# One inference step of a two-layer conv/RWKV-7 decoder on one Trainium2 core: four edits (order of the first activations, where two DVE products are kept, when a chunk and some norms are filled in, how the final squares are summed)

## The chip, the cores and the metric

The kernel runs on one core of one Trainium2 chip. The metric is the time of one execution on the device in microseconds (us). The median of three runs of the kernel before is 2742.42 us (2741.14 to 2746.84). The engines are called PE (matrix products), ACT (activations), DVE (vector), POOL (GpSimd) and SP (issues most DMAs) here, as the profile calls them.

## What is computed

1040 prompt tokens (16 learned meta tokens, then 1024) and 8 decoding tokens pass two layers of width 1024. Layer 0 mixes tokens by a Conformer convolution, layer 1 by RWKV-7; behind each stands an MLP of width 4096 with a squared ReLU, and at the end an RMS norm.

```python
def _wkv7_step(S, inp):                       # one token of RWKV-7, S is 64 x 64 for each of 16 heads
    r_t, w_t, k_t, v_t, kk_t, a_t = inp
    sa = jnp.einsum('bhvk,bhk->bhv', S, -kk_t)
    S = (S * w_t[:, :, None, :] + sa[..., None] * (kk_t * a_t)[:, :, None, :]
         + v_t[..., None] * k_t[:, :, None, :])
    y = jnp.einsum('bhvk,bhk->bhv', S, r_t)
    return S, y
...
    for i in range(DEPTH):                    # DEPTH = 2
        hn = _rmsnorm(h, norm_mix[i])
        if i % N_MIXERS == 0:
            out, buf = _conformer_conv(hn, conv_bufs[j], *[p[j] for p in conv_params])
        else:
            out, sh, S = _rwkv7(hn, shift_bufs[j], wkv_states[j], *[p[j] for p in rwkv_params])
        h = h + out
        h = h + _sqrelu_mlp(_rmsnorm(h, norm_mlp[i]), w_mlp_in[i], w_mlp_out[i])
    return (_rmsnorm(h, norm_final), ...)     # and the new states
```

One of the further outputs, conv_sample, is for each of the 8 decoding sequences the last 30 rows of its convolution buffer: 29 rows of the old state and one new row.

## The kernel before

**Matrix products.** Activations lie with the model dimension on the partitions, 128 of it at a time (KT = 8 blocks), and the tokens in three groups of about 350 columns (352, 348 or 328). Each 1024 x 128 column block of a weight comes by one DMA of 512 KB on SP's queue, in the order in which the program uses them. ACT makes a rounded high part of it (L157, "_hi"), POOL the remainder in four pieces of 128 x 256 (L162, "_lo"). Activations are split in the same way (hn_h and hn_l, m_h and m_l, z_h and z_l, hh and hl). Each product is then three matmuls (L187 high by high, L188 high by low weight, L189 low by high weight), 24 to an output block of 1024 inputs. L354 on DVE adds the output blocks of an MLP ("out") to the residual h.

**Start.** transpose_x loads the first token group, takes its mean square, loads a table of vectors (pvec, tiles stg and ptp), and makes the normalised, transposed activations: PE transposes and scales in one (L486, tile tn), ACT writes hn_h (L488), DVE hn_l (L489). Then pw1 streams the first convolution weights, pg_m (gate) and pa_m (value) in turn, through products ps_g and ps_a. A scheduler of the framework, which goes by its own model of times, orders the instructions here.

**RWKV prompt.** The 1040 tokens go in 17 chunks (16 chunks of 64 tokens and the meta tokens). For every group of chunks inverses() inverts unit triangular 32 x 32 blocks by back substitution on DVE: the blocks ni come by DMA from d_n, then for each column j one product tt (L1172) and one addition to ni (L1173), 30 of each, then ni goes to d_p (L1177) and returns transposed as p (L1200). front() of a chunk loads it and, on DVE, transposes it once more into x (L1203). PE's gg (L1257) is the first product that needs x; behind it come bT, W, po, U, S and Y of the chunk. Products of a group's output projection (ps_oo, residual add L1548) and of its MLP (ps_in, out) are the dense work of the time.

**What sets the order there.** The dense work runs under in_order(): instructions keep the order in which the Python code emits them. A filler() is called between and inside the dense products; it takes further generators in turn (the chunks, the decode step after DL = 74 points, the norms and gates of two token groups) so that each is spread evenly over its points. A generator's yield value is the number of points that it asks to be left alone.

**Decode.** decode_step works the 8 x 16 states as 16 pieces Sdec of 128 x 256. Per piece, DVE does nine instructions (L1406 to L1414): product into t4, reduce to sa, decay of Sdec, product into t4, add (L1410), product into t4, add (L1412), product into t4, reduce to yd. The trace calls the tile t4 "t". Tile t4 lies in SBUF.

**End.** final(g) squares the eight blocks of h on ACT, adds the squares up to two sums (acc_f) on POOL and DVE (L230), sums over partitions with matmuls of one column (L1569, tile fs; two records of the profile each), and takes root and reciprocal (os). PE transposes h (pf), ACT and DVE scale the two halves of a 128-token output tile ot (L1588, L1590), SP stores the tile with one DMA (L1592, L1594). final(1) runs inside the last MLP, final(2) after it.

Eight DMAs on ACT's queue (L1640) copy the old part of conv_sample from DRAM to DRAM. They depend on nothing, and the scheduler issues them in the first 21 us.

Of the kernel before, what the change touches and what calls it, by code (L numbers as in the profile page):

```python
# [8 lines left out]
F32 = mybir.dt.float32  # L9
F32R = mybir.dt.float32r  # L10
# [6 lines left out]
P = 128  # L17
D = 1024
# [30 lines left out]
def hybrid_step(tc, x_prompt, x_sample, state_conv, state_shift, state_wkv, meta_tokens,  # L49
# [10 lines left out]
    with ctx:  # L60
# [9 lines left out]
        for i, e in enumerate((RMS_EPS, LN_EPS, GN_EPS)):  # L70
            nc.vector.memset(eps_t[:, i:i + 1], e)

# [316 lines left out]
        with ExitStack() as l0:  # L389
# [53 lines left out]
            def load_vecs(tiles):  # L443

                for i in tiles:
                    st = cur["raw"].tile([P, D], F32, name=f"stg{i}", tag="raw")[:, :P]
                    nc.gpsimd.memset(st, 0.0)
                    for q, (name, ap) in enumerate(v for v in vecs if col[v[0]] // P == i):
                        r = col[name] % P
                        (nc.gpsimd if q % 2 else nc.scalar).dma_start(st[r:r + ap.shape[0], :], ap)  # L450
                    pt = bank("ptp")
                    nc.tensor.transpose(pt[:, :P], st, ident)
                    nc.vector.tensor_copy(pvec[:, i * P:(i + 1) * P], pt[:, :P])
# [9 lines left out]
            def transpose_x(g, ah, al):  # L463
                n = G0[g][1]
                tiles = load_x(xin, g)
# [12 lines left out]
                if g == 0:  # L478
                    load_vecs([0])
# [13 lines left out]
            def pw1(g, act, fill):  # L493
                n, npr = G0[g][1], prompt_of(g)
                for m in range(KT):
                    wg = load_col(conv_w_pw1[0], KT + m, f"pg{g}_{m}", nc.gpsimd)
                    wa = load_col(conv_w_pw1[0], m, f"pa{g}_{m}", nc.gpsimd)
# [12 lines left out]
                    fill()  # L510
# [26 lines left out]
            def conv_dec(c, c_col):  # L537
# [5 lines left out]
                for m in range(KT):  # L543
# [7 lines left out]
                    nc.vector.tensor_mul(win, win, wdw[:, m:m + 1, :].broadcast_to([P, DEC, CW]))  # L551
                    rd = decp.tile([P, DEC], F32, name=f"rd{m}", tag="rd")
# [119 lines left out]
            with ExitStack() as s:  # L672
# [7 lines left out]
                for _ in transpose_x(0, *acts[0]):  # L680
                    pass
                load_dw()
                for g in range(3):
# [11 lines left out]
                    pw1(g, acts[g], both)  # L695
# [464 lines left out]
        def inverses(c, n):  # L1160
# [7 lines left out]
            top = META if c == 0 else 32  # L1168
            for j in range(top - 2, 0, -1):
                wd = top - 1 - j  # L1170
                o = wk.tile([P, 256], F32, name=f"tt{c}_{j}", tag="tt")[:B, :j * wd].rearrange("p (s t) -> p s t", t=wd)
                nc.vector.tensor_mul(o, ni[:, :j, j:j + 1].broadcast_to([B, j, wd]), ni[:, j:j + 1, j + 1:top].broadcast_to([B, j, wd]))  # L1172
                nc.vector.tensor_add(ni[:, :j, j + 1:top], ni[:, :j, j + 1:top], o)  # L1173
                if j % 4 == 0:
                    yield 1.5
# [55 lines left out]
        fronts = {}  # L1231

# [11 lines left out]
        def chunk(c):  # L1244
# [6 lines left out]
            xa, bk, nr, no, p32, x32 = chunks.pop(c)  # L1251

# [124 lines left out]
        def decode_step():  # L1377

            with ExitStack() as s:
# [135 lines left out]
        with ExitStack() as l1:  # L1515
# [36 lines left out]
            def final(g):  # L1552
                lo, n = G2[g]
                hv = hl[g][:, :, :n]
                accs = mean_parts(hv, n, f"f{g}", True, "facc")
                yield 3
                for k in range(KT):
                    if k % 2:
# [7 lines left out]
                for j, i in enumerate(starts):  # L1566
                    w = min(P, n - i)
                    for q, acc in enumerate(accs):
                        nc.tensor.matmul(ps[:w, j:j + 1], acc[:, i:i + w], ones_d[:, 0:1], start=q == 0, stop=q == 1)  # L1569
# [7 lines left out]
                for j, i in enumerate(starts):  # L1577
# [36 lines left out]
            DL, DN = 74, 90  # L1614

            def late_start(n):
                for _ in range(n):
# [4 lines left out]
                                ([late_start(DL), decode_step()], DL + DN), ([norm_gates(GN_OF[1]), ng2], NGA))  # L1622
# [16 lines left out]
            for q in range(DEC):  # L1639
                nc.scalar.dma_start(o_conv_sample[0, q, 0:CB - 1, :], state_conv[0, q, 1:CB, :])  # L1640
# [46 lines left out]
```

## Time and profile before

| | |
|---|---|
| median of 3 runs | 2742.42 us |
| the profiled execution | 2743.3 us |
| its span, from the first to the last instruction of the trace | 2741.6 us |
| PE busy | 2631.0 us (96%) |
| DVE, ACT, POOL busy | 1727.8, 1124.0, 1455.6 us (63%, 41%, 53%) |
| mean granted clock of PE | 0.983 |
| DMA | 412.30 MB, 150 GB/s in the mean |

The span lies 1.7 us below the time of the same execution; what is taken out of the trace comes out of both. Rows of the trace read: start, duration, engine, line, operation, output<-inputs, shape, count, and in brackets how long the engine had been idle before and what it waited for. A table by stretches of time gives the busy time of each engine in them, then PEclk, the granted clock, and what the DMA engines did. "PEld" is the weight load of a matmul, which overlaps with matmuls.

### The profile page before, as it was taken

The page shows a single profiled execution, that of the slowest core. Times are in us where ns is not written, and L with a number is a line of the kernel's source. Part 1 is how long each engine was busy: PE and PEld are TensorE (multiplying, and loading weights), DVE is VectorE, ACT ScalarE, POOL GpSimd, SP SyncE. Part 2 cuts the span into 40 slices and gives each one's busy share as a digit, 9 for nine tenths or more (in the row PEclk, how much of TensorE's full clock was granted, in tenths as well). Part 3 has the DMA queues.
Part 4 walks back from the last instruction along what each step waited for, and adds up shares of the span by engine and source line. Part 5 has one row for each costly group of instructions (what it writes and reads, how often), then busy time and mean ns, then how long its engine had stood idle before and what let it go on. Part 6 is the DMA issues. An engine that isn't in the chain of part 4 may idle for free. (4 is left out here: it accounts for less than half of the span.)

```text
span 2741.6 us, 51590 instructions
## 1 busy us (share of the span) xinstructions
PE 2631.0 (96%) x19876; PEld 2489.7 (91%) x19876; DVE 1727.8 (63%) x3552; ACT 1124.0 (41%) x2097; POOL 1455.6 (53%) x2060
## 2 busy tenths in 40 slices
PE   8999999999999999998999999869998999999998
PEld 7999999999999999787887787768998999999998
DVE  5999999997445445335657466576679754334445
ACT  5546445445444333332434444434543542222223
POOL 6677878878887775022111113455677663333331
PEclk9999999999999999999999999989999999999999
DMA  6663544554456443667777768776675642222211
GB/s 182 170 185 113 163 138 125 158 174 131 142 159 192 138 139 101 184 198 198 202 189 203 189 166 196 192 192 163 176 234 165 166 130 87 66 69 70 70 55 43
DMA packets 624389, 412.30 MB, mean 150 GB/s; under 512 B 121656, under 2 KB 567288, under 8 KB 624142
## 3 DMA queue, kind: packets, MB, share of 16 engines
q1 hardware_dynamic: 543228, 358.60, 46.9%
q10 hardware_dynamic: 72386, 24.56, 4.2%
q0 software_dynamic: 8528, 25.83, 2.9%
q8 instruction: 157, 2.57, 0.4%
q14 instruction: 90, 0.74, 0.1%
HBM read 345.76 MB, written 64.07 MB: 149 GB/s over the span
## 5 line engine op out<-in xcount | busy, mean ns | idle before, releaser
L162 POOL TENSOR_TENSOR wo_lo<-wo_raw,wo_hi 128x256 fp32r<-128x256 f32 x736 | 546.7, 777 | 316.0 <-ACT wo_hi L157 314.2
L162 POOL TENSOR_TENSOR wi_lo<-wi_raw,wi_hi 128x256 fp32r<-128x256 f32 x640 | 472.1, 772 | 252.9 <-ACT wi_hi L157 244.4
L187 PE MATMUL out<-hh,wo_hi 128*128 128x352 f32 (+2 forms) x1536 | 501.5, 326 | 21.8 <-DVE h L354 12.8
L187 PE MATMUL ps_in<-m_h,wi_hi 128*128 128x352 f32 (+2 forms) x1536 | 494.3, 322 | 1.1 <-DVE h L354 1.1
L188 PE MATMUL out<-hh,wo_lo 128*128 128x352 f32 (+2 forms) x1536 | 495.2, 322 | 0.0
L189 PE MATMUL out<-hl,wo_hi 128*128 128x352 f32 (+2 forms) x1536 | 494.2, 322 | 0.0
L354 DVE TENSOR_TENSOR h<-h,out 128x352 f32<-128x352 f32 (+2 forms) x768 | 385.5, 510 | 171.7 <-PE out L189 170.1
L189 PE MATMUL ps_in<-m_l,wi_hi 128*128 128x352 f32 (+2 forms) x1536 | 492.2, 321 | 0.7 <-DVE m_l L285 0.7
L188 PE MATMUL ps_in<-m_h,wi_lo 128*128 128x352 f32 (+2 forms) x1536 | 491.8, 320 | 0.0
L524 DVE SCALAR_TENSOR_TENSOR cv<-u,wdw,cv 128x352 f32<-128x352 f32 (+2 forms) x720 | 377.8, 572 | 0.8
L157 ACT CAST wo_hi<-wo_raw 128x1024 fp32r<-128x1024 f32 x184 | 192.9, 1048 | 340.1 <-PE out L189 175.2
L157 ACT CAST wi_hi<-wi_raw 128x1024 fp32r<-128x1024 f32 x160 | 167.8, 1049 | 396.4 <-PE out L189 180.4
L187 PEld LDWEIGHTS out<-hh,wo_hi 128*128 128x128 f32 x1536 | 291.9, 190 | 27.9 <-DVE h L354 14.7
L188 PEld LDWEIGHTS out<-hh,wo_lo 128*128 128x128 f32 x1536 | 291.6, 190 | 0.8
L187 PEld LDWEIGHTS ps_in<-m_h,wi_hi 128*128 128x128 f32 x1536 | 289.4, 188 | 2.7 <-issue 1.3
L189 PEld LDWEIGHTS out<-hl,wo_hi 128*128 128x128 f32 x1536 | 290.5, 189 | 0.0
L189 PEld LDWEIGHTS ps_in<-m_l,wi_hi 128*128 128x128 f32 x1536 | 288.6, 188 | 1.9 <-DVE m_l L285 1.3
L188 PEld LDWEIGHTS ps_in<-m_h,wi_lo 128*128 128x128 f32 x1536 | 288.7, 188 | 0.9
L342 DVE SCALAR_TENSOR_TENSOR ps_in<-ps_in,rs_m 128x352 f32<-128x352 f32 (+2 forms) x192 | 100.2, 523 | 241.0 <-PE ps_in L189 240.6
L141 DVE TENSOR_TENSOR hl<-ps_in,hh 128x352 fp32r<-128x352 f32 (+2 forms) x192 | 98.6, 514 | 117.8 <-ACT hh L140 117.8
L343 ACT ACTIVATE ps_in<-ps_in 128x352 f32<-128x352 f32 (+2 forms) x192 | 85.0, 443 | 135.0 <-DVE ps_in L342 134.8
L1052 POOL DMA_DIRECT2D d_n<-n x32 | 24.6, 768 | 211.3 <-DVE n L1042 141.7
(361 smaller groups left out, 4823.3 us busy)
## 6 DMA issues: line engine op xcount, KB each, us to landing
wi_raw<-in_w_mlp_in_dram SPq DMA_DIRECT2D x160, 512.0 KB
wo_raw<-in_w_mlp_out_dram SPq DMA_DIRECT2D x160, 512.0 KB
wk_raw<-in_rwkv_w_k_dram SPq DMA_DIRECT2D x32, 512.0 KB
wr_raw<-in_rwkv_w_r_dram SPq DMA_DIRECT2D x32, 512.0 KB
wv_raw<-in_rwkv_w_v_dram SPq DMA_DIRECT2D x32, 512.0 KB
d_ab<-ab POOLq DMA_DIRECT2D x32, 512.0 KB, 4.6
pg_raw<-in_conv_w_pw_dram SPq DMA_DIRECT2D x24, 512.0 KB
pa_raw<-in_conv_w_pw_dram SPq DMA_DIRECT2D x24, 512.0 KB
```

What stands on the lines that cost most here:

```text
L141: eng_lo.tensor_sub(lo, src, hi.bitcast(F32))
L157: nc.scalar.copy(hi[:, :a * b], raw[:, :a * b])
L162: eng_lo.tensor_sub(lo[:, cs], raw[:, cs], hi[:, cs].bitcast(F32))
L187: nc.tensor.matmul(ps, w[0], act[0], start=first, stop=False)
L188: nc.tensor.matmul(ps, w[1], act[0], start=False, stop=False)
L189: nc.tensor.matmul(ps, w[0], act[1], start=False, stop=last)
L342: nc.vector.scalar_tensor_tensor(s, s, 0.0, rs()[:, :n], op0=ALU.max, op1=ALU.mult)
L343: nc.scalar.activation(s, s, AF.Square)
L354: nc.vector.tensor_add(hv[:, 4 * i + m, :], hv[:, 4 * i + m, :], ps[:, :n])
L524: nc.vector.scalar_tensor_tensor(acc[m][:, :n], ug[:, m, j:j + n], wdw[:, m, j:j + 1], acc[m][:, :n], op0=ALU.mult, op1=ALU.add)
L1052: nc.gpsimd.dma_start(d_n[ch0:ch0 + ncg, p].rearrange("c r t -> r c t"), n32[:, :ncg])
```

## The change

Lines of the kernel after are 1 to 28 higher than those of before (L1173 is L1192 there, L285 is L286, L1548 is L1570).

**Start.** A square root whose result nothing reads is done right after the constants, so that ACT's table for it is loaded first. The vectors' DMAs are issued ahead of the tokens' (stage_vecs, place_vecs). The first column pg_0 is loaded inside transpose_x, pa_0 behind it, and on ACT the order of this part is that of the code. The eight DRAM copies on ACT's queue are gone; in their place SP stores the 29 old rows per block from the tile sd, in which the state lies anyway, during the convolution's decode part.

**Inverses.** For the last group of chunks the product is written to one bank of PSUM ("aside") instead of an SBUF tile of its own.

**Filler.** Chunk 13 yields HOLD = 8 after its front, so what follows is emitted eight points later. The norms of the second group get a late start of NL = 16 points.

**Decode.** Tile t4 lies in a bank of PSUM.

**End.** In final(1) and final(2) each square is kept in a tile, and PE sums the eight of them: 24 matmuls to a group instead of 6, and no additions on POOL and DVE. Each half of an output tile has its own DMA.

```diff
+        nc.scalar.activation(eps_t[:, 3:4], eps_t[:, 0:1], AF.Sqrt)
...
-            def transpose_x(g, ah, al):
+            def transpose_x(g, ah, al, between=lambda: None):
                 n = G0[g][1]
+                staged = stage_vecs(0) if g == 0 else None
                 tiles = load_x(xin, g)
...
                 if g == 0:
-                    load_vecs([0])
+                    place_vecs(0, staged)
+                between()
                 dg = stat(f"dg{g}", "acc0", 1)
...
+            def pw1_weights(g, m):
+                yield load_col(conv_w_pw1[0], KT + m, f"pg{g}_{m}", nc.gpsimd)
+                yield load_col(conv_w_pw1[0], m, f"pa{g}_{m}", nc.gpsimd)
...
+                    nc.sync.dma_start(o_conv_sample[0, m, 0:CB - 1, :], sd[m // 4][m % 4 * CB + 1:(m % 4 + 1) * CB])
...
-                for _ in transpose_x(0, *acts[0]):
-                    pass
+                ready = []
+                first = pw1_weights(0, 0)
+                with tc.manual_schedule(engines={nc.scalar.engine}):
+                    for _ in transpose_x(0, *acts[0], lambda: ready.append(next(first))):
+                        pass
+                    ready.append(next(first))
...
+            aside = bank(f"tt{c}", "x")[:B] if c + n == NCH else None
             for j in range(top - 2, 0, -1):
                 wd = top - 1 - j
-                o = wk.tile([P, 256], F32, name=f"tt{c}_{j}", tag="tt")[:B, :j * wd].rearrange("p (s t) -> p s t", t=wd)
+                o = aside if aside is not None else wk.tile([P, 256], F32, name=f"tt{c}_{j}", tag="tt")[:B]
+                o = o[:, :j * wd].rearrange("p (s t) -> p s t", t=wd)
...
+        HOLD = 8
...
             xa, bk, nr, no, p32, x32 = chunks.pop(c)
+            if c == NCH - 4:
+                yield HOLD
...
-                    t4 = rows(dk.tile([P, HV * HS], F32, name=f"t4{hv}", tag="t4"))
+                    t4 = rows(bank(f"t4{hv}", "x")[:, :HV * HS])
...
-                accs = mean_parts(hv, n, f"f{g}", True, "facc")
-                yield 3
+                if g:
+                    accs = [(actp, actp2)[g - 1].tile([P, cur["wide"]], F32R, name=f"fq{g}{k}", tag=f"acth{k}").bitcast(F32)
+                            for k in range(KT)]
+                else:
+                    accs = mean_parts(hv, n, f"f{g}", True, "facc")
+                    yield 3
                 for k in range(KT):
+                    if g:
+                        nc.scalar.activation(accs[k][:, :n], hv[:, k, :], AF.Square)
...
-                        nc.tensor.matmul(ps[:w, j:j + 1], acc[:, i:i + w], ones_d[:, 0:1], start=q == 0, stop=q == 1)
+                        nc.tensor.matmul(ps[:w, j:j + 1], acc[:, i:i + w], ones_d[:, 0:1], start=q == 0, stop=q == len(accs) - 1)
...
-                    if np_:
-                        nc.sync.dma_start(o_y_prompt[0, c:c + np_, :], ot[:np_, :])
-                    if np_ < w:
-                        nc.sync.dma_start(o_y_sample.rearrange("b t d -> (b t) d"), ot[np_:w, :])
+                        if np_:
+                            nc.sync.dma_start(o_y_prompt[0, c:c + np_, cs], ot[:np_, cs])
+                        if np_ < w:
+                            nc.sync.dma_start(o_y_sample.rearrange("b t d -> (b t) d")[:, cs], ot[np_:w, cs])
...
-            DL, DN = 74, 90
+            DL, DN, NL = 74, 90, 16
...
-                                ([late_start(DL), decode_step()], DL + DN), ([norm_gates(GN_OF[1]), ng2], NGA))
+                                ([late_start(DL), decode_step()], DL + DN), ([late_start(NL), norm_gates(GN_OF[1]), ng2], NGA + NL))
...
-            for q in range(DEC):
-                nc.scalar.dma_start(o_conv_sample[0, q, 0:CB - 1, :], state_conv[0, q, 1:CB, :])
```

**The order on ACT at the start.** From the cast of the first weight on, ACT's rows were these before (pg_m_hi and pa_m_hi are casts of weights, hn_h the first activations):

```order
L157 CAST pg_0_hi<-pg_0_raw 128x1024
L1640 DMA out_dram<-in_state_conv_dram 16x1856 x2
L438 ACTIVATE ss_2_154<-ss_2_154,eps_t 96x1
L157 CAST pa_0_hi<-pa_0_raw 128x1024
L1640 DMA out_dram<-in_state_conv_dram 16x1856 x2
L157 CAST pg_1_hi<-pg_1_raw 128x1024
L1640 DMA out_dram<-in_state_conv_dram 16x1856
L488 ACTIVATE hn_h<-tn_0_216,pvec 128x352
L488 ACTIVATE hn_h<-tn_1_222,pvec 128x352
L488 ACTIVATE hn_h<-tn_2_228,pvec 128x352
L488 ACTIVATE hn_h<-tn_3_234,pvec 128x352
L488 ACTIVATE hn_h<-tn_4_240,pvec 128x352
```

In the changed kernel the rows at the same place are:

```order
L158 CAST pg_0_hi<-pg_0_raw 128x1024
L496 ACTIVATE hn_h<-tn_0_228,pvec 128x352
L496 ACTIVATE hn_h<-tn_1_234,pvec 128x352
L496 ACTIVATE hn_h<-tn_2_240,pvec 128x352
L496 ACTIVATE hn_h<-tn_3_246,pvec 128x352
L496 ACTIVATE hn_h<-tn_4_252,pvec 128x352
L496 ACTIVATE hn_h<-tn_5_258,pvec 128x352
L496 ACTIVATE hn_h<-tn_6_264,pvec 128x352
L496 ACTIVATE hn_h<-tn_7_270,pvec 128x352
L158 CAST pa_0_hi<-pa_0_raw 128x1024
L158 CAST pg_1_hi<-pg_1_raw 128x1024
L158 CAST pa_1_hi<-pa_1_raw 128x1024
```

The eight hn_h went ahead of the casts of pa_0, pg_1 and pa_1 (before, the last three hn_h stood behind that of pa_1); the order on PE is the same in both.

**The order on PE around the last inverse.** Before, the last matmuls of output block 6 of the projection (ps_oo_6), the chunk's gg and bT, and the first matmul of block 7:

```order
L187 MATMUL ps_oo_6_20121<-z_h_19656,wo_6_hi 128x328
L188 MATMUL ps_oo_6_20121<-z_h_19656,wo_6_lo 128x328
L189 MATMUL ps_oo_6_20121<-z_l_19664,wo_6_hi 128x328
L1257 MATMUL gg_20149<-x_19921,no_19775 32x32 x16
L1275 MATMUL bT_20173<-ident,bk_19770 128x128 x4
L1275 MATMUL bT_20179<-ident,bk_19770 128x128 x4
L187 MATMUL ps_oo_7_20189<-z_h_19649,wo_7_hi 128x328
```

In the changed kernel the same gg stands behind block 2 of the MLP's first product:

```order
L188 MATMUL ps_in_2_0_20270<-m_h_20145,wi_0_2_hi 128x328
L189 MATMUL ps_in_2_0_20270<-m_h_20145,wi_0_2_lo 128x328
L190 MATMUL ps_in_2_0_20270<-m_l_20153,wi_0_2_hi 128x328
L1279 MATMUL gg_20304<-x_19893,no_19758 32x32 x16
L1297 MATMUL bT_20328<-ident,bk_19753 128x128 x4
L1297 MATMUL bT_20334<-ident,bk_19753 128x128 x4
L188 MATMUL ps_in_3_0_20349<-m_h_20138,wi_0_3_hi 128x328
```

Between ps_oo_6 and gg there now are 24 matmuls each of ps_oo_7, ps_in_0, ps_in_1 and ps_in_2, and four short ones of st_m, the mean square for the MLP's norm.

**The order on DVE there.** Before, the end of the inverse, the transposed x and the low parts m_l of the MLP's input:

```order
L1173 TENSOR_TENSOR ni_19509<-ni_19509,tt_2_19595 128x2x29
L1172 TENSOR_TENSOR tt_1_19598<-ni_19509 128x30
L1173 TENSOR_TENSOR ni_19509<-ni_19509,tt_1_19598 128x30
L1548 TENSOR_TENSOR h_0_19647<-h_0_19647,ps_oo_6_20121 128x328
L1203 STREAM_TRANSPOSE x_19921<-p_19776 128x256
L1269 TENSOR_SCALAR p_20169<-p_19776,par32q 128x8x32 x2
L285 SCALAR_TENSOR_TENSOR m_l_20225<-h_0_19647,pvec,m_h_20217 128x328
```

In the changed kernel m_l comes first (the other four m_l follow the last row shown, and then x, L1222):

```order
L1191 TENSOR_TENSOR tt_19523<-ni_19521 128x58
L1192 TENSOR_TENSOR ni_19521<-ni_19521,tt_19523 128x2x29
L1570 TENSOR_TENSOR h_0_19630<-h_0_19630,ps_oo_6_20082 128x328
L1191 TENSOR_TENSOR tt_19523<-ni_19521 128x30
L1192 TENSOR_TENSOR ni_19521<-ni_19521,tt_19523 128x30
L286 SCALAR_TENSOR_TENSOR m_l_20146<-h_0_19630,pvec,m_h_20138 128x328
L286 SCALAR_TENSOR_TENSOR m_l_20147<-h_0_19630,pvec,m_h_20139 128x328
L286 SCALAR_TENSOR_TENSOR m_l_20148<-h_0_19630,pvec,m_h_20140 128x328
L286 SCALAR_TENSOR_TENSOR m_l_20149<-h_0_19630,pvec,m_h_20141 128x328
L1570 TENSOR_TENSOR h_0_19630<-h_0_19630,ps_oo_7_20110 128x328
```

So all of m_l moved from behind x to in front of it, directly behind the last row of the inverse.

More of the change, by code (lines that the diff above doesn't have):

```diff
@@ L445, in load_vecs, with stage_vecs, place_vecs @@
                 for i in tiles:
[L446 to L453, printed above, removed]
+                    place_vecs(i, stage_vecs(i))
+            def stage_vecs(i):
+                st = cur["raw"].tile([P, D], F32, name=f"stg{i}", tag="raw")[:, :P]
+                nc.gpsimd.memset(st, 0.0)
+                for q, (name, ap) in enumerate(v for v in vecs if col[v[0]] // P == i):
+                    r = col[name] % P
+                    (nc.gpsimd if q % 2 else nc.scalar).dma_start(st[r:r + ap.shape[0], :], ap)
+                return st
+            def place_vecs(i, st):
+                pt = bank("ptp")
+                nc.tensor.transpose(pt[:, :P], st, ident)
+                nc.vector.tensor_copy(pvec[:, i * P:(i + 1) * P], pt[:, :P])
             def load_dw():
@@ L491, in transpose_x, with pw1 @@
                     yield 1
-            def pw1(g, act, fill):
+            def pw1_weights(g, m):
+                yield load_col(conv_w_pw1[0], KT + m, f"pg{g}_{m}", nc.gpsimd)
+                yield load_col(conv_w_pw1[0], m, f"pa{g}_{m}", nc.gpsimd)
+            def pw1(g, act, fill, ready=()):
                 n, npr = G0[g][1], prompt_of(g)
+                ws = chain(ready, chain.from_iterable(pw1_weights(g, m) for m in range(len(ready) // 2, KT)))
                 for m in range(KT):
-                    wg = load_col(conv_w_pw1[0], KT + m, f"pg{g}_{m}", nc.gpsimd)
-                    wa = load_col(conv_w_pw1[0], m, f"pa{g}_{m}", nc.gpsimd)
+                    wg, wa = next(ws), next(ws)
                     pg = dense(wg, act, n, f"g{g}_{m}", fill)
@@ L694, in both @@
                             nxt()
-                    pw1(g, acts[g], both)
+                    pw1(g, acts[g], both, [] if g else ready)
                     for _ in tail:
```

## The prediction, made before the changed kernel ran

> **What bounds the kernel.** I read the page first, then PE's waits, then a table of stretches. The busy times and the two lines of the chain that ended last:
>
> ```profile
> PE 2631.0 (96%) x19876; PEld 2489.7 (91%) x19876; DVE 1727.8 (63%) x3552; ACT 1124.0 (41%) x2097; POOL 1455.6 (53%) x2060
> PE 26%; DVE 6%; DMA 2%; issue 1%; POOL 0%; ACT 0%; SPq 0%; ACTq 0%; DVEq 0%; POOLq 0%
> ```
>
> PE is the bound: of the span of 2741.6 us it idles 110.6. The change leaves PE's matrix work as it is but for some small matmuls, so a gain can only come out of these 110.6 us. Whom PE waits for (us in total, times, longest):
>
> ```profile
> PE gg L1257 <- DVE x L1203: 16.1, 1, 16.1
> PE out L187 <- DVE h L354: 12.8, 9, 2.3
> PE out L187 <- DVE hl L141: 8.8, 4, 3.4
> PE tn L486 <- DVE hn_l L489: 5.7, 1, 5.7
> ```
>
> Where the idle time lies, by stretches of 30 us (busy time and instructions of PE, its weight loads, DVE, ACT, POOL; granted clock, DMA share, GB/s):
>
> ```profile
> 0.00:30.00 30.00, 17.16 (x88) 15.70 (x89) 9.49 (x28) 15.27 (x24) 15.81 (x31) 0.85 0.71 199
> 1800.00:1830.00 30.00, 25.74 (x270) 23.93 (x269) 29.38 (x54) 12.87 (x22) 24.38 (x27) 0.94 0.84 210
> 1830.00:1860.00 30.00, 14.02 (x104) 13.29 (x105) 15.10 (x37) 12.02 (x23) 8.84 (x14) 0.72 0.36 95
> 2040.00:2070.00 30.00, 27.80 (x182) 26.99 (x181) 29.62 (x62) 10.04 (x14) 25.40 (x31) 1.00 0.54 159
> 2070.00:2100.00 30.00, 27.85 (x172) 27.08 (x171) 29.11 (x64) 10.71 (x16) 23.49 (x30) 0.94 0.57 166
> 2100.00:2130.00 30.00, 25.86 (x167) 24.83 (x167) 29.62 (x58) 10.48 (x15) 22.48 (x29) 1.00 0.53 158
> 2130.00:2160.00 30.00, 25.39 (x149) 24.84 (x149) 25.66 (x52) 14.31 (x26) 19.50 (x26) 0.89 0.70 189
> 2700.00:2730.00 30.00, 29.77 (x202) 29.04 (x200) 19.58 (x40) 14.02 (x31) 5.97 (x6) 1.00 0.09 36
> ```
>
> The edits fall on four of these places: the start (12.8 us idle), the last inverse (16.0 in 1830 to 1860), the decode step (2.2, 2.2, 4.1 and 4.6, together 13.1, with DVE full), and the end, where PE is full and every added matmul costs.
>
> **A, the start.** The timeline of PE, ACT and POOL:
>
> ```profile
> 12.84 4.23 PE L486 MATMUL tn<-dg,xt 128*128 128x128 f32 x30
> 18.88 1.04 ACT L157 CAST pa_hi<-pa_raw 128x1024 fp32r<-128x1024 f32 x1 [5.61 <-DMA pa_raw<-in_conv_w_pw_dram]
> 20.00 2.77 POOL L162 TENSOR_TENSOR pa_lo<-pa_raw,pa_hi 128x256 fp32r<-128x256 f32 x4 [4.02 <-ACT pa_hi L157]
> 21.58 2.33 ACT L488 ACTIVATE hn_h<-tn,pvec 128x352 fp32r<-128x352 f32 x5
> 22.80 4.15 PE L486 MATMUL tn<-dg,xt 128*128 128x128 f32 x18 [5.72 <-DVE hn_l L489]
> 27.87 0.66 PE L187 MATMUL ps_g<-hn_h,pg_hi 128*128 128x352 f32 x1
> ```
>
> PE had 5 of 8 tn tiles done at 17.07, but ACT sat behind the cast of pa_0, whose data landed at 18.88, and reached the first hn_h only at 21.58. With the activations ahead of the casts, hn_h runs at 0.47 each (2.33 / 5) beside PE; the remaining 18 tn follow at 17.1 and take 2.5 us at the pace of the first 30 (0.14), so the last hn_h ends near 19.7, and the first dense matmul comes at about 20.3 instead of 27.87: 7.5 us. What is late next is pa_0: its cast waits for the eight hn_h, to 19.7 at most 0.8 later than now, its low part is done at about 23.7, and PE needs it after 24 matmuls of ps_g (0.16 to 0.29 each, so 24 to 27). It just fits. The table load and the vectors' DMAs go into time in which ACT waits for the first tokens, at nothing. The eight new stores come during the convolution's decode part, behind weights that are loaded ahead; at nothing too, and the copies that they replace no longer share DMA with the first loads. If that cover is gone, pa_0 is late (rival 3). Range 4 to 9.5.
>
> **B, the last inverse.** The rows of PE and DVE around the 16.1 us, one line grouped over 1791 to 1837 us, and the same operation on 240 elements twice:
>
> ```profile
> L1173 DVE TENSOR_TENSOR ni<-ni,tt 128x30 f32<-128x30 f32 (+14 forms) x30 | 15.3, 509 | 0.5
> 1814.00 0.92 DVE L1173 TENSOR_TENSOR ni<-ni,tt 128x240 f32<-128x240 f32 x1
> 1817.13 0.39 DVE L1173 TENSOR_TENSOR ni<-ni,tt 128x240 f32<-128x240 f32 x1
> 1829.60 0.32 PE L189 MATMUL ps_oo<-z_l,wo_hi 128*128 128x328 f32 x1
> 1836.36 0.19 DVE L1173 TENSOR_TENSOR ni<-ni,tt 128x30 f32<-128x30 f32 x1
> 1845.39 0.45 DVE L1203 STREAM_TRANSPOSE x<-p 128x256 f32<-128x256 f32 x1 [8.44 <-DMA p<-d_p]
> 1845.98 1.06 PE L1257 MATMUL gg<-x,no 32*32 32x32 f32 x32 [16.07 <-DVE x L1203]
> 1846.98 1.97 PE L1275 MATMUL bT<-ident,bk 128*128 128x128 f32 x8
> 1850.96 2.68 DVE L285 SCALAR_TENSOR_TENSOR m_l<-h,pvec,m_h 128x328 fp32r<-128x328 f32 x5 [0.26 <-ACT m_h L284]
> 1853.26 0.31 PE L187 MATMUL ps_in<-m_h,wi_hi 128*128 128x328 f32 x1
> ```
>
> PE ends ps_oo_6 at 1829.75 and waits through the end of the inverse (1836.55) and the way of ni through DRAM and back (8.84 us to x). Then gg and bT run at half clock (1.06 and 1.97), and ps_oo_7 begins cold, so that the MLP starts at 1853.26. Two edits act. First, the 96 matmuls moved ahead of gg (0.15 each, 14.4 us) fill the wait. Second, DVE's time: the same addition takes 0.39 or 0.92. Between 0.19 at 30 elements and 0.39 at 240, the 30 additions would sum to 9.6 undisturbed; they took 15.3, so 5.7 us are stretch. With the product in PSUM the addition has one input in SBUF, and such operations do not stretch in the trace:
>
> ```profile
> L1217 DVE TENSOR_TENSOR xa<-A,m_ar x68: 405/418/430, 1303.7 to 1960.1; 64x256 f32<-64x256 f32 x68
> L1219 DVE TENSOR_TENSOR nr<-A,m_ar x68: 406/416/426, 1304.5 to 1960.4; 128x256 f32<-128x256 f32 x68
> ```
>
> (smallest, median, largest ns; A lies in PSUM). So the inverse ends at about 1830.9; the product itself still reads ni twice from SBUF and stays stretched. New wait: ps_in_0 needs all eight m_l, which now stand behind the inverse on DVE. Eight at 0.54 and the residual add come to 4.8, up to 8.5 if the m_l stretch, so 1835.7 to 1839.4. PE has ps_oo_7 and ps_in_0 (7.2 us from 1829.75) until 1837: at most 2.5 us idle. Then ps_in_1, ps_in_2 and gg at about 1846, when x has long landed (1830.9 + 8.8 = 1839.7). gg comes no earlier than before, but 96 matmuls are done, and about 2 us of half clock are saved: 16. On SP the loads of p come ahead of weights that stood in front of them; these wait for the inverse with p, and since it ends earlier they are issued no later than before. The held chunk and the late norms only move work of DVE and PE by one to two output blocks; the norms' readers, the next group's projection, are far behind. But the chunks from 13 on get three output blocks fewer to hide their chain of DVE steps in; I take 2 off for that: **14**. If the inverse ends as late as before, 5.7 are lost, and if the chain shows its waits again, more: range 6 to 18.
>
> **C, the decode step.** Smallest, median and largest of the two additions that now read t4 from PSUM, then their sums:
>
> ```profile
> L1410 DVE TENSOR_TENSOR Sdec<-Sdec,t x16: 407/690/881, 2033.0 to 2137.8; 128x256 f32<-128x256 f32 x16
> L1412 DVE TENSOR_TENSOR Sdec<-Sdec,t x16: 408/759/961, 2034.4 to 2140.2; 128x256 f32<-128x256 f32 x16
> L1412 DVE TENSOR_TENSOR Sdec<-Sdec,t 128x256 f32<-128x256 f32 x16 | 11.1, 691 | 0.3
> L1410 DVE TENSOR_TENSOR Sdec<-Sdec,t 128x256 f32<-128x256 f32 x16 | 10.9, 682 | 0.2
> ```
>
> Unstretched, 32 at 0.41 make 13.1 instead of 22.0, so DVE saves 8.9 us where it is full (29.6, 29.1 and 29.6 of 30) and PE's idle time, 10.3 of it before out for h, follows from that. The five other operations that read two SBUF tiles stay. Not all that DVE saves reaches PE: **6**, range 0 to 9.
>
> What t4 in PSUM costs DVE elsewhere the trace does not show for this tile: the two reductions read it, four products write it. The nearest rows are L1217 and L1219, 0.42 with one PSUM input against 0.41 with none, so 0.01. The Trainium skill, "Perfetto Trace Analysis", section "Optimizing Scalar/DVE Operations", speaks against this change: it gives an access overhead of about 60 ns to DVE on SBUF and about 125 on PSUM. By it the eight instructions per piece that touch t4 would cost 0.065 each, an estimate of 8.3 us in all, which would eat C's saving, and 3.9 us for 60 in the inverse. The 0.41 and 0.42 of this trace do not bear it out.
>
> **D, the end.** The final sums, and the rows behind the last square:
>
> ```profile
> L1569 PE MATMUL fs<-ones_d,acc_f 128*128 128x1 f32 (+1 forms) x24 | 2.9, 234 | 0.1
> 2730.05 0.48 ACT L225 ACTIVATE sq_f<-h 128x352 f32<-128x352 f32 x1
> 2731.14 1.17 PE L1569 MATMUL fs<-ones_d,acc_f 128*128 128x1 f32 x10
> 2732.35 0.41 ACT L1574 ACTIVATE os<-fs,eps_t 128x2 f32<-128x2 f32 x2 [1.20 <-PE fs L1569]
> ```
>
> A matmul of this kind is two records, 2.9 / 12 = 0.24 us. final(1) gets 18 more on a full PE: +4.3. In final(2), 17 of the 24 stand behind the last square: 2730.5 + 4.1 = 2734.6 before the root, which now starts at 2732.35: +2.3. The half DMAs start a little earlier, and POOL's and DVE's additions go: −0.6. Together **+6**, range +2 to +8.
>
> **The sum** is −7.5 − 14 − 6 + 6 = −21.5. From the profiled execution's 2743.3 that gives 2721.8; the median before, 2742.4, is 0.9 below that execution, so I say **2721**. The four ranges added as independent errors give about ±9.
>
> **Rivals.**
> 1. *The wait only moves.* DVE is full at 29.38 of 30 before the wait; if other work of its queue takes the 5.7 us, m_l ends at 1841 to 1845, and if the three last chunks then show their chain, B is worth 6. In the same way C may give 2, since PE waits for the last add of an output block whatever stands before it. −7.5 − 6 − 2 + 6 = −9.5: 2733. For it speaks that PE's waits follow DVE's order here.
> 2. *PSUM eats what it saves.* If each of the 128 instructions of the decode step that touch t4 takes 0.07 us longer (8.9 / 128), C is nothing, and 60 in the inverse lower B by 4.2: −7.5 − 9.8 + 6 = −11.3, so 2730. Against it: 0.42 beside 0.41 in the rows above. By the skill's figure just named it would come out about there.
> 3. *The start gives its gain back*, because pa_0 and the next columns come too late behind the activations: PE waits 5 us in ps_a_0. Then A is 2.5, the time 2726.
> 4. *Slower:* the same with a dearer access. With p more for each of these 188 instructions, all on a full DVE whose delay then passes to PE in full, the sum is −7.5 − (14 − 60 p) − (8.9 − 128 p) + 6 = −24.4 + 188 p. It turns at p = 0.13; at p = 0.2 it is +13: 2755. The rows show 0.01, but on an input; a product that DVE writes to PSUM stands nowhere alone in them.
>
> **How the numbers follow.** The forecast (2712 to 2730) gets 0.60; rival 1 0.18, rival 2 0.07, rival 3 0.08, rival 4 0.07. Rivals 2 and 3 lie at the forecast's upper edge; to hold 8 in 10 the range takes in rival 1 and the added ranges: 2706 to 2737. A difference of 0.2% (5.5 us) is about what a measurement can tell from none. Of rival 1 about a third would lie within it, of rival 4 a small part: faster 0.86, same 0.08, slower 0.06.
>
> **What the changed profile would show.** A: hn_h in one run of eight before the cast of pa_0, the first dense matmul near 20 us, no wait of ps_a for pa_lo. B: no idle of 16 us before gg; L1192 at 0.19 to 0.42 throughout, L1191 still up to 1.1; a wait of at most 3 us in ps_in_0 for m_l; the granted clock at 1.00 from 1830 to 1860. C: L1432 and L1434 at 0.41, PE's waits for h halved in the stage. D: fs with 48 records in each of two groups and a root that starts some 2 us later behind the last square. I am wrong if L1192 still stretches, if the chunks after 13 make PE wait for W, U or Y, or if DVE's products into PSUM take longer than into SBUF.

## The result, and the profile after

The changed kernel took 2751.93 us, the median of 13 runs (2748.31 to 2759.84), beside 2748.09 of 13 runs of the kernel before (2741.14 to 2761.67). The ratio is 1.0016, with a 95% interval from 1.0004 to 1.0029: slower, by less than a fifth of a per cent, where 21 us of gain were forecast. The profiled execution took 2754.32 us with a span of 2752.6, 11.0 more than the span before.

The busy times and the lines of the chain that ended last:

```profile
PE 2645.0 (96%) x19948; PEld 2496.7 (91%) x19948; DVE 1715.7 (62%) x3546; ACT 1122.3 (41%) x2097; POOL 1441.4 (52%) x2054
PE out L188 4%; PE out L189 4%; PE out L190 4%; PE ps_in L188 3%; PE ps_in L190 3%; PE ps_in L189 3%; POOL wo_lo L163 1%; DVE h L355 1%; DMA d_z<-ez 1%; DMA wo_raw<-in_rwkv_w_o_dram 0%; DVE acc_m L261 0%; PE fs L1597 0%; DVE tt L1191 0%; DVE t L1431 0%; PE pv L908 0%
```

In the chain a weight split of POOL (wo_lo) has come in, and the inverse's ni, named there before, is gone. PE's waits tell more:

```profile
PE pw L559 <- ACT win L561: 15.1, 1, 15.1
PE out L188 <- DVE hl L142: 12.7, 9, 3.4
PE out L188 <- DVE h L355: 5.8, 6, 1.6
PE ps_in L190 <- DVE m_l L286: 5.3, 9, 2.7
```

The waits that the change aimed at are gone (gg for x, 16.1 us) or smaller (out for h, 12.8 to 5.8). One grew, out for hl, from 8.8 to 12.7; 2.6 of that lie in the stretch shown next. A new one of nearly the same size has come in another place: pw, the convolution's decode part of layer 0. What happened there, by stretches of 10 us (PE, its loads, DVE, ACT, POOL, clock, DMA share, GB/s):

```profile
300.00:310.00 10.00, 10.00 (x65) 9.98 (x64) 7.29 (x16) 1.50 (x3) 3.06 (x6) 1.00 0.18 61
310.00:320.00 10.00, 6.85 (x32) 5.85 (x30) 4.99 (x11) 1.85 (x3) 2.93 (x5) 0.83 0.22 70
320.00:330.00 10.00, 0.00 (x0) 0.00 (x0) 0.02 (x1) 0.00 (x0) 0.00 (x0) 0.63 0.57 179
330.00:340.00 10.00, 5.28 (x20) 5.28 (x21) 4.99 (x11) 3.25 (x6) 5.87 (x9) 0.52 0.38 119
```

From 320 to 330 us no compute engine does anything (DVE is busy for 0.02 us). The timeline tells who is late, from SP through ACT to PE:

```profile
298.19 14.54 SPq L564 DMA_DIRECT2D out_dram<-sdec  x4
...
313.10 1.04 ACT L158 CAST wi_hi<-wi_raw 128x1024 fp32r<-128x1024 f32 x1 [9.24 <-DMA wi_raw<-in_w_mlp_in_dram]
...
332.32 1.04 ACT L158 CAST wo_hi<-wo_raw 128x1024 fp32r<-128x1024 f32 x1 [17.35 <-DMA wo_raw<-in_w_mlp_out_dram]
...
334.72 0.66 PE L559 MATMUL pw<-ident,sdec 120*128 120x120 f32 x2 [15.11 <-ACT win L561]
```

SP spends 14.54 us on the issue of four of the new stores of conv_sample (L564, 29 rows of 4 KB each, 116 KB). The weights behind them land 9.24 and 17.35 us after ACT is ready; the rest, win and pw too, waits in line behind ACT's cast. What the DMA engines moved from 296 to 312 us, in 40 slices:

```profile
GB/s 20 31 31 20 31 20 31 138 124 243 340 343 199 46 20 31 72 20 31 20 31 20 31 31 20 31 20 31 20 31 31 20 31 20 31 20 31 20 22 22
```

But for one weight it is about 26 GB/s. In the trace's packets exactly one of 4096 bytes is under way for 92% of this time, at 0.159 us each: 8 x 29 of them make 36.9 us.

To place all of it, I compared when the same instruction starts in both traces (additions to h, L354 and L355, by their number; at 1764 us the chunks' xa). The lag is that of the changed kernel behind the one before; the third column is that of experiment e2_split_16_13, told below, in which only the stores' shape differs:

| at (us, before) | lag, changed | lag, stores in two parts | stage between |
|---|---|---|---|
| 290 | −11.5 | −7.4 | A, start |
| 374 | +13.4 | −7.5 | the stores |
| 1764 | +20.1 | −8.0 | layer 0, projections, chunks |
| 2043 | +7.1 | −21.0 | B, last inverse |
| 2160 | −4.9 | −33.1 | C, decode step |
| 2331 | +2.9 | −25.5 | next projection |
| end of span | +11.0 | −17.2 | D, end |

The two traces are of single executions, that of before 4.8 us below the median of its runs and that of the changed kernel 2.4 above, so the lag at the end is 11.0 where the medians differ by 3.8. The stores cost 24.9 us. Of the further 6.7 lost up to 1764 us in the changed kernel, the run with the other stores shows nothing (the lag changes by −0.5). Nine further runs with the same code in that stage lie between −2.1 (e8) and +6.1 (e7), so most of it may be scatter between executions; it stays open.

### The profile page after: what moved, and what is told of

Its sections match the earlier page's. It is cut to its first block, busy times and chain, and to the rows that moved or that the text cites. A ratio compares the mean times of both kernels' runs of the same rounds, so it can differ in the third digit from the quotient of the medians.

```text
span 2752.6 us, 51712 instructions
## 1 busy us (share of the span) xinstructions
PE 2645.0 (96%) x19948; PEld 2496.7 (91%) x19948; DVE 1715.7 (62%) x3546; ACT 1122.3 (41%) x2097; POOL 1441.4 (52%) x2054
## 5 line engine op out<-in xcount | busy, mean ns | idle before, releaser
L188 PE MATMUL out<-hh,wo_hi 128*128 128x352 f32 (+2 forms) x1536 | 502.8, 327 | 19.0 <-DVE hl L142 12.7
L355 DVE TENSOR_TENSOR h<-h,out 128x352 f32<-128x352 f32 (+2 forms) x768 | 385.4, 511 | 166.7 <-PE out L190 164.6
L536 DVE SCALAR_TENSOR_TENSOR cv<-u,wdw,cv 128x348 f32<-128x348 f32 (+2 forms) x720 | 377.9, 574 | 0.7
```

The costliest lines, as they stand in the source:

```text
L188: nc.tensor.matmul(ps, w[0], act[0], start=first, stop=False)
L355: nc.vector.tensor_add(hv[:, 4 * i + m, :], hv[:, 4 * i + m, :], ps[:, :n])
L536: nc.vector.scalar_tensor_tensor(acc[m][:, :n], ug[:, m, j:j + n], wdw[:, m, j:j + 1], acc[m][:, :n], op0=ALU.mult, op1=ALU.add)
```

## The experiments

Each run's ratio is to runs of the kernel before on the same chip, with its 95% interval.

**e1_copies_back**: the changed kernel with the copies on ACT's queue again.

```diff
-                    nc.sync.dma_start(o_conv_sample[0, m, 0:CB - 1, :], sd[m // 4][m % 4 * CB + 1:(m % 4 + 1) * CB])
...
+            for q in range(DEC):
+                nc.scalar.dma_start(o_conv_sample[0, q, 0:CB - 1, :], state_conv[0, q, 1:CB, :])
```

> The changed kernel with one edit undone: the old rows of conv_sample are copied from DRAM to DRAM on ACT's queue again, and the eight stores of 29 rows on SP are gone. Theory 1 (each store of 29 rows runs at about 27 GB/s, one DMA engine's pace, and the weights queued behind them wait): the markers between 290 and 345 us, which lost 25 us in the changed kernel, lose under 2; the whole comes to about 22 us below the kernel before, ratio 0.990 to 0.994. Theory 2 (the stall comes from the shifted order of weights, casts and transposes in that stretch, not from the stores): the stall at 315 to 335 us stays within 5 us, ratio about 1.00. In both the copies come back to the start, which may cost up to 4 us of the 11.5 gained there.

Measured: 2733.99 us, 0.9954 (0.9939 to 0.9969). The stall is gone (lag −0.4 at 290 us, −0.5 at 374), so the stores caused it. But the whole gain of the start is gone as well, 11 us where at most 4 had been expected, though ACT's new order is still there. ACT's timeline, and PE's first dense matmul:

```profile
19.26 2.97 ACTq L1667 DMA_DIRECT2D out_dram<-in_state_conv_dram  x2
22.28 2.33 ACT L496 ACTIVATE hn_h<-tn,pvec 128x352 fp32r<-128x352 f32 x5 [7.88 <-DMA out_dram<-in_state_conv_dram]
...
28.58 0.66 PE L188 MATMUL ps_g<-hn_h,pg_hi 128*128 128x352 f32 x1
```

hn_h stands first in the order and still starts only at 22.28, behind the issue of the last two copies on its own queue.

**e2_split_16_13**: the changed kernel with each store in two parts.

```diff
-                    nc.sync.dma_start(o_conv_sample[0, m, 0:CB - 1, :], sd[m // 4][m % 4 * CB + 1:(m % 4 + 1) * CB])
+                    r = m % 4 * CB + 1
+                    nc.sync.dma_start(o_conv_sample[0, m, 0:16, :], sd[m // 4][r:r + 16])
+                    nc.sync.dma_start(o_conv_sample[0, m, 16:CB - 1, :], sd[m // 4][r + 16:r + CB - 1])
```

> The changed kernel with each store of 29 rows made as two, of 16 and of 13 rows, on the same queue at the same place. Theory 1 (the shape keeps the store on one DMA engine): the two parts spread over 16 and 13 engines, the rate in that stretch goes from 27 to over 100 GB/s, and the stall goes: ratio to the kernel before 0.988 to 0.993. Theory 1b (a store on SP's queue holds up the weights behind it, whatever its shape): 25 us of stall stay, ratio 1.000 to 1.006.

Measured: 2725.42 us, 0.992 (0.9905 to 0.9935). The same bytes from the same place on the same queue cost nothing. What DMA moved from 290 to 302 us, in 40 slices:

```profile
GB/s 316 326 319 248 167 154 109 150 82 218 396 287 300 246 246 287 222 169 155 138 177 263 311 365 386 386 270 231 157 157 157 225 253 341 369 382 294 212 116 102
```

And the stretch in which all engines had stood still:

```profile
320.00:330.00 10.00, 10.00 (x66) 9.98 (x65) 9.66 (x22) 4.83 (x10) 7.83 (x12) 1.00 0.52 153
```

From 296 us on only the stores have packets of 4096 bytes in this stretch, and up to 14 of them are now under way at once. So it is the number of rows. The Trainium skill, "DMA: Bandwidth & Descriptors", section "Why a DMA increments its semaphore by 16 and not by 1", states the rule: a DMA uses the largest number of engines up to 16 that divides the slowest dimension of both its sides. By it 29 rows get one engine, 16 rows 16 and 13 rows 13; one packet at a time against up to 14 agrees.

**e3_store_act_queue**: the stores of 29 rows, issued by ACT (`nc.scalar.dma_start` in L564).

> The changed kernel with the eight stores of 29 rows on ACT's queue in place of SP's. If the stores only block SP's queue by standing in it, the stall goes (ratio 0.988 to 0.993). If one DMA engine is what is scarce, the weights still need that engine, which now serves two queues: the weights' share on it halves, and 5 to 20 of the 25 us stay (ratio 0.993 to 1.000).

Measured: 2751.1 us, 1.0014 (1.0005 to 1.0024), lag −10.8 at 290 us and +13.3 at 374. Taking the stores off SP's queue gives nothing back. From the timelines of SP and ACT:

```profile
303.28 15.93 SPq L147 DMA_DIRECT2D wo_raw<-in_w_mlp_out_dram  x2
...
303.60 10.91 ACTq L564 DMA_DIRECT2D out_dram<-sdec  x2
```

SP's queue now holds weights alone, and still the issue of two of them takes 15.93 us (4.19 for two in the kernel before, at the same place). This fits weights that need all engines, also the one that the stores fill. ACT stands behind its own issues as well, 10.91 us for two stores. The second expectation had the direction; it allowed up to 20 of the 25 us to stay, and 24.1 stayed.

**e4_before_plus_stores**: the kernel before with the stores of 29 rows in place of the copies.

> The kernel before with that one edit alone: eight stores of 29 rows on SP in the convolution's decode part in place of the copies on ACT's queue. Theory 1: 20 to 25 us lost near 300 to 340 us, less 1 to 4 gained at the start, where the copies no longer share DMA with the first loads: ratio 1.006 to 1.009. Theory 2: within 0.002 of the kernel before.

Measured: 2771.82 us, 1.0091 (1.0075 to 1.0107). Alone, the edit costs 25 us, the upper end of what was expected; the gain at the start did not come (first dense matmul at 28.07 us).

The next five (e5 to e8 and e10) start from e2_split_16_13 and undo one further part each.

**e5_inverse_in_sbuf** and **e6_no_hold**: the two halves of B.

```diff
-            aside = bank(f"tt{c}", "x")[:B] if c + n == NCH else None
+            aside = None
...
-            if c == NCH - 4:
-                yield HOLD
```

> The changed kernel with the conv_sample stores in two parts (16 and 13 rows, ratio 0.992 to the kernel before), and the product of the last inverse in SBUF again. Theory (the additions stretch while POOL reads SBUF, and the inverse ends the stage): the 30 additions go from about 9.6 back to about 15 us, PE waits 4 to 6 us more for m_l behind the inverse: ratio 0.9935 to 0.9945. Rival (what moved gg behind 96 matmuls gave all of it, and m_l waits for its own input): within 2 us of that kernel, 0.992 to 0.993.

> The same base, without the 8 points that chunk 13 yields, so that gg stands right behind ps_oo_6 again. Theory: PE waits for x again, about 10 us (16 of the kernel before less what the faster inverse saves), part of which later chunks give back: 6 to 11 us slower than the base, ratio 0.994 to 0.996. Rival (the hold only shifts the wait to the chunks behind it): within 3 us of the base, 0.991 to 0.993.

Measured: 2732.88 us, 0.9939 (0.9922 to 0.9957), and 2736.82, 0.9959 (0.9948 to 0.997). With the product in SBUF the marker behind the inverse comes 4.0 us later than in the base, and the additions took 13.6 us for the 29 in the stretch asked for; the changed kernel's 30 take 9.6, the product keeps its stretch:

```profile
L1191 DVE TENSOR_TENSOR tt<-ni 128x30 f32<-128x30 f32 (+14 forms) x30 | 14.4, 481 | 4.9 <-DMA ni<-d_n 4.4
L1192 DVE TENSOR_TENSOR ni<-ni,tt 128x30 f32<-128x30 f32 (+14 forms) x30 | 9.6, 321 | 0.6
```

Without the hold PE waits for x again:

```profile
PE gg L1279 <- DVE x L1224: 12.3, 1, 12.3
```

Both parts act, and about as sized: some 5 and some 11 us by the ratios. They do not simply add up, since both shorten the same wait. The intervals of e5 and of the base overlap, so e5 rests on its trace.

**e7_decode_in_sbuf**: t4 in SBUF.

```diff
-                    t4 = rows(bank(f"t4{hv}", "x")[:, :HV * HS])
+                    t4 = rows(dk.tile([P, HV * HS], F32, name=f"t4{hv}", tag="t4"))
```

> The same base, with t4 of the decode step in SBUF again. Theory (the two additions stretch by about 0.28 us each, 9 us on a full DVE): PE's waits between 2040 and 2160 us grow by 8 to 12, but the next projection, whose weights and z were late in the changed kernel, gives 4 to 7 of them back: 2 to 6 us slower than the base, ratio 0.9928 to 0.9942. Rival (t4 in PSUM cost as much as it saved): within 1 us, 0.9918 to 0.9923.

Measured: 2737.77 us, 0.9968 (0.9956 to 0.9981), 12 us above the base, more than either theory said. The two additions in the changed kernel, then in this run:

```profile
L1432 DVE TENSOR_TENSOR Sdec<-Sdec,t x16: 403/412/422, 2040.8 to 2147.3; 128x256 f32<-128x256 f32 x16
L1434 DVE TENSOR_TENSOR Sdec<-Sdec,t x16: 405/410/421, 2042.6 to 2149.1; 128x256 f32<-128x256 f32 x16
```

```profile
L1434 DVE TENSOR_TENSOR Sdec<-Sdec,t x16: 411/547/918, 2015.4 to 2132.0; 128x256 f32<-128x256 f32 x16
L1436 DVE TENSOR_TENSOR Sdec<-Sdec,t x16: 411/553/960, 2017.6 to 2134.1; 128x256 f32<-128x256 f32 x16
```

Its lag behind the base grows by 9.1 us from 2020 to 2113 us; about 3 us of lag stood there already before the decode step, and no edit of this run explains them. The 4 to 7 us that the next projection was to give back did not come: that loss is in this run as well, so it has another cause (e9).

**e8_old_end** and **e10_whole_stores**: the end as before, and only the output DMAs as before.

```diff
-                if g:
+                if g > 5:
...
-                            nc.sync.dma_start(o_y_prompt[0, c:c + np_, cs], ot[:np_, cs])
+                        nc.sync.dma_start(o_y_prompt[0, c:c + np_, :], ot[:np_, :])
```

(The first edit, at both places of final, stands in e8 alone; the second, with its line for o_y_sample, in both.)

> The same base, with the end as before: sums of squares by POOL and DVE, one DMA for an output tile. Theory (18 more one-column matmuls in final(1) on a full PE, 17 behind the last square in final(2), and output tiles that wait for their stores): 6 to 8 us faster than the base, ratio 0.989 to 0.990. Rival (the additions on DVE and POOL cost as much as the matmuls): within 2 us, 0.991 to 0.993.

> Stores of conv_sample in two parts (ratio 0.992), squares still summed by TensorE, but one DMA for each output tile. It splits the 8.5 us that the new end costs. Theory: the added matmuls cost 4.3 + 2.3 of it and the half stores, behind whose output tiles PE waits 1.4 us, the rest: 1 to 2.5 us faster than the base, ratio 0.991 to 0.9917. Rival (the half stores are the larger part): 4 us or more faster, under 0.9905.

Measured: 2718.45 us, 0.9889 (0.9873 to 0.9906), and 2725.7, 0.9917 (0.9902 to 0.9931). The old end is 7 to 8.5 us faster, and nearly all of it goes with the squares on PE; by the medians the half stores cannot be told from none. (In the profiled execution of e10 PE waits for no output tile, where it waited 1.4 us in the base; but the granted clock there is 0.57 to 0.58 from 2694 to 2698 us, right behind the sums, against 1.00 in the base. So a small gain of the whole stores may be hidden.) In the changed kernel's timeline the sums stand in two runs, each of 34 records, and the root of final(2) comes 4.0 us after the second run's start:

```profile
2720.36 3.42 PE L1597 MATMUL fs<-ones_d,fq 128*128 128x1 f32 x34
2739.97 3.99 PE L1597 MATMUL fs<-ones_d,fq 128*128 128x1 f32 x34
2743.99 0.41 ACT L1602 ACTIVATE os<-fs,eps_t 128x2 f32<-128x2 f32 x2 [5.08 <-PE fs L1597]
```

**e9_old_end_norms_early**: e8 without the late start of the second group's norms.

```diff
-                                ([late_start(DL), decode_step()], DL + DN), ([late_start(NL), norm_gates(GN_OF[1]), ng2], NGA + NL))
+                                ([late_start(DL), decode_step()], DL + DN), ([norm_gates(GN_OF[1]), ng2], NGA))
```

> Stores of conv_sample in two parts, the end as before (ratio 0.989), and the second group's norms without their late start. If the late norms are what makes the next projection wait for z and its weights (about 2 us of PE's waits between 2160 and 2200), 1 to 3 us faster: 0.988 to 0.9886. If they free DVE for the chunks and the decode step, 1 to 5 us slower: 0.9893 to 0.991.

Measured: 2714.91 us, 0.9876 (0.9857 to 0.9895). The lag at the next projection (2160 to 2331 us) grows by 2 to 4 us, depending on the block of the stage before from which it is counted, instead of 7.6 in e2 and 7.4 in e8. So the late norms made about half of that loss or more. Some of it they had given before, in the decode step: from 2043 to 2160 us the lag falls by 10.8 in e8 and by 8 to 10 in e9. Against e8 the intervals overlap: the sign of the sum is not settled. It is the fastest version that I ran, 1.2% faster than the kernel before.

**e11_before_split_stores** and **e13_before_stores_taps_split**: the kernel before with the stores in two parts and no new order of the activations; and the same with the load of the 31 rows of convolution taps (wst) in two parts. **e12_best_taps_split**: e9 with that load in two parts.

```diff
-                nc.scalar.dma_start(wst, conv_w_dw.rearrange("l w c -> (l w) c"))
+                nc.scalar.dma_start(wst[:16], conv_w_dw.rearrange("l w c -> (l w) c")[:16])
+                nc.scalar.dma_start(wst[16:CW], conv_w_dw.rearrange("l w c -> (l w) c")[16:CW])
```

> The kernel before with one edit: the copies of conv_sample on ACT's queue replaced by the stores in two parts on SP, without the new order of the activations. It tells what gave the 9 to 11 us at the start. Theory (ACT stood behind the issue of copies on its own queue until 22 us, so their going is the gain): the first dense matmul comes at 21 to 23 us, 5 to 7 us earlier than before, ratio 0.9975 to 0.9982. Rival (the order of activations ahead of casts gives it): the first dense matmul stays past 25 us, ratio 0.999 to 1.000.

> The kernel before with the stores in two parts and the taps' load in two parts, without the new order of the activations. Theory (in the run without the taps' split the tokens came at 11 us instead of 6 because 31 rows stood ahead of them on one DMA engine): PE's first wait for tokens falls from 11 to about 6 us, and the first dense matmul comes at 22 to 25 us, behind the casts that stand ahead of the activations on ACT: ratio 0.997 to 0.999. Rival (the tokens were late for another reason): the first wait stays at 11 us, ratio 0.9995.

> The best version so far (stores in two parts, the end as before, norms without the late start; ratio 0.9876), and the load of the 31 rows of convolution taps made as two, of 16 and 15 rows. Theory (a transfer of 31 rows also runs on one DMA engine, 5 us at 27 GB/s): the single-engine stretch at 10 to 16 us goes, and the weights in the queue behind it land earlier: 0 to 3 us faster, 0.9865 to 0.9876. Rival: the start does not wait for that engine, within 1 us of 0.9876.

Measured: e11 2746.49 us, 0.9995 (0.9985 to 1.0006); e13 2744.42, 0.9985 (0.9971 to 1.0); e12 2716.42, 0.9883 (0.9862 to 0.9904). PE's wait for the first tokens in e11, then in e13:

```profile
PE tx L470 <- DMA xt<-in_x_prompt_dram: 12.3, 2, 11.2
```

```profile
PE tx L471 <- DMA xt<-in_x_prompt_dram: 5.9, 3, 5.3
```

And the first dense matmul of e11, then of e13:

```profile
28.20 0.43 PE L187 MATMUL ps_g<-hn_h,pg_hi 128*128 128x352 f32 x1
```

```profile
21.66 0.43 PE L187 MATMUL ps_g<-hn_h,pg_hi 128*128 128x352 f32 x1
```

In e11 the scheduler had put the taps' 31 rows ahead of the tokens. They too went one packet at a time (27 packets of 4096 bytes on ACT's queue from 1 to 11 us, never more than two at once), and the tokens waited. So the rival's figures for e11 came true, but not for its reason: with 16 and 15 rows the first dense matmul comes at 21.66 us with the old order of the activations. The cast of pa_0, which waited until 18.88 us in the kernel before, runs earlier there:

```profile
12.77 1.03 ACT L157 CAST pa_hi<-pa_raw 128x1024 fp32r<-128x1024 f32 x1
```

With the new order, the first dense matmul comes between 19.90 (the changed kernel) and 22.84 us (e8) where the copies are gone and the taps are whole, and at 28.58 with the copies (e1): with this order the copies cost 6 to 9 us. With the old order e13 gains 6 us, but it drops the copies and splits the taps at once, and in the kernel before the taps too are loaded between the first weights (L457, at 6.48 us); no run separates the two. The new order itself adds little: the lag at 290 us is −8.3 in e13 and −6.6 to −11.5 with the new order. e12 shows no gain over e9: with the taps behind the tokens, their split is worth nothing that could be measured.

## Why the prediction was wrong, point by point

**The step that failed** is the sentence in A: "The eight new stores come during the convolution's decode part, behind weights that are loaded ahead; at nothing too". They cost 24.9 us: 29 rows went one packet at a time, at about 26 GB/s, and the weights behind them came late; in 16 and 13 rows the same bytes cost nothing (e2). I had counted the stores and their place in the queue, and not the rows of one transfer. The trace before has no store of this shape, so the cost could not be put at nothing without a bound. It does have a load of 31 rows, the taps: their packets of 4096 bytes go one after the other there, 31 in 6.3 us (9.8 to 16.1 us), so a sign of it stood in the trace. A price was at hand too: at 43 GB/s, the lowest rate in the page's 40 slices, the 928 KB (950,272 bytes) take 22 us. That is no bound from above, for the stores ran slower still, but it would have put a loss of this size into the range.

**A, the start** (7.5): 7.4 in e2, 11.5 in the changed kernel, 6.6 to 10.8 in eight other runs that have the new order and no copies. The size was about right, and that is luck, for the reason was not: the order of the activations alone gives nothing (e1), and e13 gains nearly as much without it. The row of the cast at 18.88, which waited for pa_0, was read rightly. But I put the going of the copies at no value of its own, and with the new order it is their issue on ACT's queue that holds the activations until 22.28 us. What made pa_0 late in the kernel before, the copies or the taps' 31 rows, stays open.

**B, the inverse** (14): 13.0 in both columns. The mechanism was right in both halves: additions with one input in PSUM took 9.6 us, the sum forecast from undisturbed rows, and PE's wait for x went. PE's longest wait for m_l there was 2.7 us, for which at most 2.5 was forecast.

**C, the decode step** (6): mis-sized. The two additions fell to 0.41 us, 22.0 to 13.2 us, as forecast. In e7 the additions sum to 20.1 us and the four products to 41.8, beside 13.2 and 38.4 in its base: 10.3 us of DVE, of which 9.1 reach PE's markers. I had counted the additions alone, and had taken a third off because "Not all that DVE saves reaches PE". On a full DVE nearly all did. (The 12 us of the table's stage hold what the late norms gave there as well.) Rivals 2 and 4 fell: the reductions that read t4 from PSUM take 0.42 (0.41 before), the products that write it sum to 38.2 us beside 41.0.

**D, the end** (+6): +8.3 by the lag and 7 to 8.5 by e8. final(1) cost about 7 by the markers where 4.3 was forecast; final(2) added 1 to 2, as forecast. In the changed kernel PE also waits once for an output tile (1.7 us), which was not in the sum. But e10, without that wait, has the same 7 (and the low clock named there), so what makes the rest of it is not settled.

None of the four rivals was it: the waits did not just move, DVE's access to PSUM cost nothing, and pa_0 was not late.

**Late norms**: I costed them at nothing. They made the next projection wait, some 4 to 6 of 7.6 us, against up to 3 that they gave before.

Without the failed step the sum was right: −21.5 forecast, −21.8 (2725.42 against 2747.19) in e2. That agreement is partly luck, since C, D and the norms were off in both directions and A came by another way.

## What to carry to other kernels

Before a transfer is moved or added, look at the number of rows of its outermost dimension: 29 or 31 rows went one packet at a time here, and the weights of 128 rows waited behind them, whichever queue issued them; a split into 16 rows and the rest costs one more issue. And when a copy "depends on nothing", it can still hold the engine on whose queue it is issued (until 22.28 us in e1): count it there before you put its going at nothing.

## What the runs showed of the hardware that I had not expected

A DMA of 29 rows of 4 KB moved about 26 GB/s, one packet of 0.159 us at a time; with 16 and 13 rows the stretch of the stores moved 242 GB/s in the mean, weights included. Issuing them from another engine changed nothing (1.0014 beside 1.0016). DVE's products into PSUM took no longer than into SBUF (38.2 us for 64 of them beside 41.0), and an addition with one input in PSUM kept 0.40 to 0.42 us beside a busy POOL, where two inputs in SBUF went up to 0.96.
